# One layout of the PSUM banks in a hybrid decoder step: row tiles and chunks in halves of bank pairs, and the last pair's additions off GpSimd

## The chip, the cores and the metric

The kernel runs on one core of one Trainium2 chip. The core has five engines with queues of their own: TensorE (PE, matmuls), VectorE (DVE), ScalarE (ACT), GpSimd (POOL) and SyncE (SP, here only an issuer of transfers). TensorE writes its sums to PSUM, eight banks of 512 float32 values in each of 128 partitions; VectorE and ScalarE read them from there. The metric is the device time of one execution in microseconds (us), as the median of several runs.

## What is computed

One layer of a decoder for 1024 prompt tokens and 8 sample tokens, 1032 columns in all, D = 2048, in float32:

```
h = rmsnorm(x, g_pre)
proj = h @ w_in
q, k, v, za, ub, zb, ga, gb = split(proj)
ya, s_ret_new = retention(q, k, v, pos, s_ret)
ya = (ya * silu(za)) @ w_pa
yb, s_re_new, s_im_new = s5(ub, s_re, s_im, ...)
yb = (yb * silu(zb)) @ w_pb
merged = sigmoid(ga) * ya + sigmoid(gb) * yb
out = merged @ w_out
return x + rmsnorm(out, g_post), s_ret_new, s_re_new, s_im_new
```

The S5 branch holds one more matrix product, `y * sigmoid(y @ w_glu + b_glu)`. The results are the output rows of both groups and the new states.

## The kernel before

Every float32 factor is split into two parts, `hi` (rounded) and `lo` (the rest), and a product is the sum of three matmuls: hi by hi, hi by lo, lo by hi. For weights this is done by `wtile` and `prep`: SP loads a block of 128 x 512, ACT casts it to `whi`, DVE subtracts to get `wlo`. Both rotate through three buffers.

The work is laid out by hand in program order; a scheduler keeps the order of each engine's queue close to it and puts in the waits. The function `emit` holds it all. Its stages, in order, with what they take from PSUM:

- Start: the first two row tiles of ub, six banks side by side, while x arrives. Then six further row tiles of ub by `linear`. A row tile is 128 output rows by 1032 columns in three thirds of 384, 384 and 264 columns, t = 0, 1, 2; each third takes one bank from `mmbank` and is read by an `evac` function as soon as its last quarter of k is done. Two row tiles of v follow in `ps2`, again six banks.
- The pairs of row tiles of the rest of w_in, then (after the GLU) of w_pa and w_pb. Two row tiles are a 2 x 2 block that is computed with seven products (n = 0 to 6) by the method of Strassen and Winograd. `product` takes a pair of banks for each of three sums, "a", "b" and "d", per step; `evac_st` or `evac_p` reads them. A step has the results "11", "22", "21" and "12": first digit the row tile, second digit the half of the columns. Small additional work is put in between as a background list `bg` (one piece at each `slot`) or at a product's number (`at`, `late_work`).
- The GLU product, eight row tiles by `linear`.
- The out projection. `out_rows` computes the columns from 640 on, 392 wide, with `linear` and `thirds=(3,)`, one bank for each of 16 row tiles. `out_tokens` computes the columns before 640 the other way round, with 128 tokens as rows: three chunks of tokens, then two, in four groups g of 512 output columns, with k in 16 steps and the chunks inside each step. `evac` squares a chunk with ACT, with a misc bank as a place to throw the squares, and multiplies it with DVE.

PSUM has two layouts. `psum_layout(("pmm", 5), ("pms", 3))` gives five single banks for `mmbank` and three for `misc`, which serves transposes and small products. `psum_layout(("pst", 3), ("pms", 2))` gives three pairs and two misc banks. The first holds from the start through the v tiles, the second from the first product to the last one, the first again in the out projection. In the second layout `mmbank` hands out one half of a pair and leaves the other half unused, so that a GLU row tile takes all three pairs.

In the last stage of the pairs, `pb`, the gated result of a pair p is added to what `pa` left in `pap_d`, in `gated`. For p of 0 and 1 the addition is made by an accumulating transfer, and the write to `mg_d` comes LAG = 4 products later. For p over 1 `load_z` loads the other part into a tile `pp` and `add` makes the sum: by DVE, in the last pair (p = 7) by GpSimd for "11", "22" and "21". The second column half of the last two pairs is kept in `last_t` and split (`mg_split`) for the out projection from there; the first half goes through `mg_d`, is loaded again by `fill` and split row by row.

Of the kernel before, what the change touches and what calls it, by code (L numbers as in the profile page):

```python
# [10 lines left out]
F32 = mybir.dt.float32  # L11
# [67 lines left out]
def emit(ctx, tc, I, O):  # L79
    nc = tc.nc  # L80
    V, A, P, T = nc.vector, nc.scalar, nc.gpsimd, nc.tensor

    def tt(out, a, b, op, eng=None):
        return (eng or V).tensor_tensor(out, a, b, op)  # L84
# [4 lines left out]
    def add(out, a, b, eng=None):  # L89
        return tt(out, a, b, ALU.add, eng)  # L90
# [20 lines left out]
    banks_of = {}  # L111

    def psum_layout(*pools):
        if "stack" in banks_of:
            banks_of.pop("stack").close()
            banks_of.clear()
        st = banks_of["stack"] = ExitStack()
        for name, bufs in pools:
            banks_of[name] = st.enter_context(tc.tile_pool(name=name, bufs=bufs, space=PSUM))

    psum_layout(("pmm", 5), ("pms", 3))
    ctx.callback(lambda: banks_of["stack"].close())
    dr = ctx.enter_context(tc.tile_pool(name="dr", bufs=1, space=DRAM))

# [81 lines left out]
    def three(ps, w, i, x, t0, t1, first, last):  # L206
# [3 lines left out]
        T.matmul(ps, wh[:, i, :], xl[:, t0:t1], start=False, stop=False)  # L210
        anchor["p"] = T.matmul(ps, wl[:, i, :], xh[:, t0:t1], start=False, stop=last).ins  # L211

    def mmbank(name="mm"):
        if "pst" in banks_of:
            return banks_of["pst"].tile([128, 2, 512], F32, name="acc")[:, 0, :]
        return banks_of["pmm"].tile([128, 512], F32, name="mm")

    def misc():
        return banks_of["pms"].tile([128, 512], F32, name="misc")
# [8 lines left out]
    def wnext(wd, m, kq):  # L228
        if (m, kq) not in ahead:
            if not todo:  # L230
                return wquarter(wd, m, kq)
            fetch_w()
        if todo:
            fetch_w()
        return ahead.pop((m, kq))

    def linear(wd, m, kt, x, evac, thirds=(0, 1, 2), tick=None):
        ps = {}
        nq = kt // 4
        for kq in range(nq):  # L240
            w = wnext(wd, m, kq)
            for t in thirds:
                t0, t1 = THIRDS[t]
                if kq == 0:
                    ps[t] = mmbank()
                for i in range(4):
                    k = 4 * kq + i
                    three(ps[t][:, 0:t1 - t0], w, i, x(k), t0, t1, k == 0, k == kt - 1)
                if kq == nq - 1:
                    evac(t, ps[t][:, 0:t1 - t0])  # L250
                if tick is not None:
                    tick(kq, t)
            slot()
# [41 lines left out]
    def x_of(k):  # L295
        return xs[k][:, 0, :], xs[k][:, 1, :]
# [49 lines left out]

    with tc.tile_pool(name="start", bufs=3) as sp:
        ssq = sp.tile([128, TOK], F32, name="ssq", bufs=1)
        banks = [[mmbank() for _ in range(3)], [mmbank(), mmbank(), misc()]]
        w = None  # L350
        sqs = deque()
        for k in range(KD):
            xr = sp.tile([128, TOK], F32, name="xr")
            xh, xl = x_of(k)
            parts = THIRDS[0:3] if k == 0 else [(0, TOK)]
            for n, (a, b) in enumerate(parts):
                nc.sync.dma_start(xr[:, a:b], I["xT"][k, :, a:b])
                if k % 4 == 0 and n == 0:
                    w = [wquarter(w_in, M_UB, k // 4)]
                if k % 4 == 0 and n == len(parts) - 1:  # L360
                    w.append(wquarter(w_in, M_UB + 1, k // 4))
                A.activation(xh[:, a:b], xr[:, a:b], AF.Copy, scale=gpre[:, k:k + 1])
                V.scalar_tensor_tensor(xl[:, a:b], xr[:, a:b], gpre[:, k:k + 1], xh[:, a:b].bitcast(F32), ALU.mult, ALU.subtract)  # L363
            if k == 0:
                A.activation(ssq, xr, AF.Square)
            else:
                sqs.append(sp.tile([128, TOK], F32, name="sq", bufs=3))
                A.activation(sqs[-1], xr, AF.Square)
            for j in range(2):
                for t, (t0, t1) in enumerate(THIRDS[0:3]):  # L370
                    three(banks[j][t][:, 0:t1 - t0], w[j], k % 4, x_of(k), t0, t1, k == 0, k == KD - 1)
            if k > 1:
                add(ssq, ssq, sqs.popleft())
        add(ssq, ssq, sqs.popleft())
        for j in range(2):
            for t, (t0, t1) in enumerate(THIRDS[0:3]):
                evac_ub_raw(j, t, banks[j][t][:, 0:t1 - t0])

        def first_rms():
            yield  # L380
            yield from rms_bcast(ssq, rstd, sp)
            for j in range(2):
                scale_ub(j)

        bg.append(first_rms())
        linear(w_in, M_UB + 2, KD, x_of, evac_ub(2))
        drain()

# [424 lines left out]
    steps = [(kh, p) for kh in range(2) for p in range(NP)] + [(kh, p) for kh in ("pa", "pb") for p in range(8)]  # L813
# [63 lines left out]
    acc = {}  # L877
# [298 lines left out]
                yield  # L1176

    bg.append(first_forms())
    ps2 = [[mmbank() for _ in range(3)], [mmbank(), mmbank(), misc()]]
    with tc.issue_after(anchor["s"]):  # L1180
        fetch(0)
    for part_ in range(2):
        for j in range(2):
            for kq in (2 * part_, 2 * part_ + 1):
# [3 lines left out]
                for t, (t0, t1) in enumerate(THIRDS[0:3]):  # L1188
                    for i in range(4):
                        k = 4 * kq + i  # L1190
# [2 lines left out]
                        evac_v(j)(t, ps2[j][t][:, 0:t1 - t0])  # L1193
                slot()
    prep(1)
    psum_layout(("pst", 3), ("pms", 2))
    k2p = {}
    TAGS = [12, 13, 14, 15] + list(range(12))
    xs = {}
# [44 lines left out]
    for s in range(2 * NP):  # L1244
        kh, p = steps[s]
# [235 lines left out]
    zq = {}  # L1481
# [3 lines left out]
    def load_z(s, name):  # L1485
        kind, p = steps[s]
        r, c = AT[name]
        zq[name] = zz_tile()
        A.dma_start(zq[name], (sga_d if kind == "pa" else sgb_d)[2 * p + r, :, HT * c:HT * c + HT])
        if kind == "pb" and p > 1:  # L1490
            zq[name, "p"] = ppp.tile([128, HT], F32, name="pp")
            A.dma_start(zq[name, "p"], pap_d[2 * p + r, :, HT * c:HT * c + HT])

    def gated(g, name, t, ps=None):
        s = g // 7
        kind, p = steps[s]
        r, c = AT[name]
        m, cols = 2 * p + r, slice(HT * c, HT * c + HT)
        z = zq.pop(name)
        if ps is None:  # L1500
            mul(t, t, z)
        else:
            mul(two(t), ps, two(z))
        if kind == "pa":
            P.dma_start(pap_d[m, :, cols], t)
        elif (name, "p") in zq:
            add(t, t, zq.pop((name, "p")), P if p == 7 and name != "12" else V)
            if c and p > 5:
                last_t[m] = t
            P.dma_start(mg_d[m, :, cols], t)  # L1510
        else:
            P.dma_start(t, pap_d[m, :, cols], accum_op=ALU.add)
            at(g + LAG, lambda: P.dma_start(mg_d[m, :, cols], t))
# [45 lines left out]
    for s in range(S0, len(steps)):  # L1559
        kind, p = steps[s]  # L1560
# [57 lines left out]
    estack.close()  # L1618
    wstack.close()
    stage_pool(SW, 3)  # L1620
    psum_layout(("pmm", 5), ("pms", 3))
    zp = ctx.enter_context(tc.tile_pool(name="zp", bufs=1))
    stl = ctx.enter_context(tc.tile_pool(name="stl", bufs=2))
    wxp = ctx.enter_context(tc.tile_pool(name="wxp", bufs=1))
# [79 lines left out]
    def out_tokens(c0, nch, last):  # L1704
# [60 lines left out]
        order_w = deque((g, k) for g in range(4) for k in range(KD))  # L1765
        w = {}
        for g in range(4):
            ps = [mmbank() if c < 2 else misc() for c in range(nch)]
            steps = [[(k, c) for c in range(nch)] for k in range(KD)]
            if last and g == 3:  # L1770
                steps[13:] = [[(k, c) for k in (13, 14, 15)] for c in range(nch)]
            for st in steps:
                for k, c in st:
                    while order_w and order_w[0] <= (g, k + 1):
                        gk = order_w.popleft()
                        w[gk] = wtile(I["w_outB"][gk])
                    wh, wl = (t.rearrange("p a b -> p (a b)") for t in w[g, k])
                    t = (c0 + c) * 128
                    xh, xl = (a[:, t:t + 128] for a in mg[k])
                    for a, b in ((xh, wh), (xh, wl), (xl, wh)):  # L1780
                        anchor["p"] = T.matmul(ps[c], a, b, start=k == 0 and a is xh and b is wh, stop=k == KD - 1 and a is xl).ins  # L1781
                    if k == KD - 1:
                        if c == 0:
                            slots[g] = free.popleft()
                            zt[g] = flat(slots[g])
                            if not last:
                                load_step(g)
                            elif g:
                                for cc in range(nch):
                                    load_x(g, cc)  # L1790
                        evac(g, c, ps[c])
                        if last and g == 3:
                            for gg in range(4):
                                finish(gg, c, A if gg % 2 else nc.sync)
                slot()
# [87 lines left out]
```

## Time and profile before

| | us |
|---|---|
| median of three runs | 2620.34 |
| lowest and highest | 2619.47, 2620.56 |
| the profiled execution | 2618.49 |
| its span, first to last instruction | 2616.7 |

The mean granted TensorE clock of the profiled execution is 0.998 of full speed. The profile is read by its page (busy time of each engine, the costliest groups of instructions, transfers), by its list of waits (for each waiting instruction what ended the wait), by its timeline (start and duration of each instruction, with the idle time before it on its engine in brackets), and by a table of windows (busy time, clock and share of transfers in each stretch). In the tiles' names buffer numbers are left out: `mm`, `misc` and `acc` are PSUM banks, `a` is a split activation, `p`, `u` and `st` are the results of a step on their way out.

### The profile page before, as it was taken

To read this page: it belongs to the slowest core of one execution; us is meant where nothing else is said; L and a number is where in the kernel's file an instruction comes from. 1 tells how busy PE (TensorE), PEld (TensorE's weight loads), DVE (VectorE), ACT (ScalarE), POOL (GpSimd) and SP (SyncE) were. 2 spreads that over 40 slices of the span, in tenths; PEclk is the share of its full clock that TensorE was granted. 3 is DMA by queue.
4 is the path that set the end of the run, shared out by engine and by line. 5 is a ranking of instruction groups with operands and counts; after the bars stand their busy time and mean duration, and the time that the engine had idled before them with its cause. 6 is when DMAs were issued, how large, how long until landed. Compare 5 with 4: busy or idle time off the path is not lost. (4 is left out here: it accounts for less than half of the span.)

```text
span 2616.7 us, 51319 instructions
## 1 busy us (share of the span) xinstructions
PE 2592.8 (99%) x19652; PEld 2531.2 (97%) x19652; DVE 1855.9 (71%) x3872; ACT 955.0 (36%) x1679; POOL 688.8 (26%) x1137
## 2 busy tenths in 40 slices
PE   9999999999999999999999999999999999999998
PEld 8999999999999999999999999999999999998886
DVE  6655988888889877558877666665577877544555
ACT  6113233333323324442234444445332422443344
POOL 0103322222222222332235433333422221111011
PEclk9999999999999999999999999999999999999999
DMA  6896534444444447887778878778867786656666
GB/s 192 262 263 213 154 114 127 138 119 121 133 122 128 131 135 237 206 207 169 166 200 242 228 188 210 200 195 248 271 217 259 231 231 212 216 167 179 188 200 228
DMA packets 229909, 500.25 MB, mean 191 GB/s; under 512 B 32432, under 2 KB 54912, under 8 KB 229536
## 3 DMA queue, kind: packets, MB, share of 16 engines
q0 software_dynamic: 90352, 263.82, 35.9%
q1 hardware_dynamic: 103072, 179.57, 22.5%
q10 hardware_dynamic: 36240, 53.60, 7.0%
q8 instruction: 154, 2.52, 0.4%
q14 instruction: 91, 0.75, 0.1%
HBM read 340.57 MB, written 156.30 MB: 190 GB/s over the span
## 5 line engine op out<-in xcount | busy, mean ns | idle before, releaser
L892 PE MATMUL acc<-a,whi 128*128 128x258 f32 x9632 | 1562.9, 284 | 1.0 <-ACT whi L873 0.6
L892 PEld LDWEIGHTS acc<-a,whi 128*128 128x128 f32 x9632 | 1326.8, 190 | 5.2 <-issue 2.4
L892 PE MATMUL acc<-a,wlo 128*128 128x258 f32 x4816 | 969.5, 283 | 0.0
L892 PEld LDWEIGHTS acc<-a,wlo 128*128 128x128 f32 x4816 | 745.1, 189 | 0.0
L84 DVE TENSOR_TENSOR wlo<-wraw,whi 128x512 fp32r<-128x512 f32 x482 | 332.3, 690 | 235.3 <-ACT whi L202 135.6
L873 ACT CAST whi<-wraw 128x512 fp32r<-128x512 f32 x344 | 213.5, 621 | 619.0 <-PE acc L892 492.5
L873 ACT CAST whi<-wr 128x512 fp32r<-128x512 f32 x258 | 160.1, 620 | 516.8 <-PE acc L892 438.1
L209 PE MATMUL mm<-a,whi 128*128 128x384 f32 (+2 forms) x704 | 233.7, 333 | 8.4 <-ACT whi L202 5.0
L210 PE MATMUL mm<-a,whi 128*128 128x384 f32 (+2 forms) x704 | 233.7, 332 | 0.0
L211 PE MATMUL mm<-a,wlo 128*128 128x384 f32 (+2 forms) x704 | 232.4, 330 | 0.0
L84 DVE TENSOR_TENSOR wlo<-wr,whi 128x512 fp32r<-128x512 f32 x273 | 187.4, 686 | 47.7 <-ACT whi L873 29.8
L1781 PE MATMUL mm<-whi,a 128*128 128x512 f32 x512 | 171.2, 395 | 0.0
L202 ACT CAST whi<-wraw 128x512 fp32r<-128x512 f32 x138 | 85.5, 620 | 210.4 <-PE mm L210 102.4
L209 PEld LDWEIGHTS mm<-a,whi 128*128 128x128 f32 x704 | 133.2, 190 | 9.1 <-ACT whi L202 5.0
L211 PEld LDWEIGHTS mm<-a,wlo 128*128 128x128 f32 x704 | 133.9, 190 | 0.4 <-DVE wlo L84 0.2
L210 PEld LDWEIGHTS mm<-a,whi 128*128 128x128 f32 x704 | 133.4, 189 | 0.4 <-DVE a L363 0.4
L84 DVE TENSOR_TENSOR wraw<-wr 128x512 f32<-128x512 f32 x172 | 118.3, 688 | 6.9 <-DMA wr<-in_w_pa 4.6
L1781 PEld LDWEIGHTS mm<-whi,a 128*128 128x128 f32 x512 | 96.2, 188 | 22.8
L84 DVE TENSOR_TENSOR p<-acc,p 128x516 f32<-128x516 f32 x86 | 59.7, 694 | 77.8 <-PE acc L892 77.6
L84 DVE TENSOR_TENSOR wlo<-wx,whi 128x512 fp32r<-128x512 f32 x76 | 52.5, 692 | 71.0 <-ACT whi L202 70.4
L84 DVE TENSOR_TENSOR u<-acc,u 128x516 f32<-128x516 f32 x86 | 59.7, 694 | 59.5 <-PE acc L892 58.2
L1781 PE MATMUL mm<-wlo,a 128*128 128x512 f32 x256 | 101.4, 396 | 0.0
(374 smaller groups left out, 3416.9 us busy)
## 6 DMA issues: line engine op xcount, KB each, us to landing
wr<-in_w_in SPq DMA_DIRECT2D x280, 256.0 KB
pt_d<-u POOLq DMA_DIRECT2D x70, 258.0 KB, 3.2
u<-pt_d POOLq DMA_DIRECT2D x70, 258.0 KB, 5.3
wraw<-in_w_outB SPq DMA_DIRECT2D x66, 256.0 KB
stg<-fm_d POOLq DMA_DIRECT2D x44, 258.0 KB, 4.3
wx<-in_w_outB SPq DMA_DIRECT2D x43, 256.0 KB
wraw<-in_w_out SPq DMA_DIRECT2D x39, 256.0 KB
pt_d<-st POOLq DMA_DIRECT2D x35, 258.0 KB, 3.4
```

Source lines behind the costliest of these rows:

```text
L84: return (eng or V).tensor_tensor(out, a, b, op)
L202: anchor["a"] = A.copy(hi, raw).ins
L209: T.matmul(ps, wh[:, i, :], xh[:, t0:t1], start=first, stop=False)
L210: T.matmul(ps, wh[:, i, :], xl[:, t0:t1], start=False, stop=False)
L211: anchor["p"] = T.matmul(ps, wl[:, i, :], xh[:, t0:t1], start=False, stop=last).ins
L873: anchor["a"] = A.copy(hi, f).ins
L892: anchor["p"] = T.matmul(ps[:, j, 0:258], a[:, i, :], b[:, 258 * j:258 * j + 258], start=first and i == 0 and a is wh and b is xh, stop=n ...
L1781: anchor["p"] = T.matmul(ps[c], a, b, start=k == 0 and a is xh and b is wh, stop=k == KD - 1 and a is xl).ins
```

## The change

One layout, three pairs and two misc banks, holds for the whole program, and the calls that switch it are gone. `mmbank` takes a pair and hands out its two halves one after the other. `linear` drops an unused half before t = 0, before t = 2 and before t = 3, so that t = 0 and 1 share a pair and the others have one for themselves. The start and the two v tiles take three whole pairs. In `out_tokens` all chunks take halves, also the third that had a misc bank; and in the part with three chunks the last two k are done chunk by chunk.

In the last pair of `pb`, "11" and "21" no longer load `pp` but take the accumulating transfer with its later write to `mg_d`; "22" is added by DVE, as "12" was.

```diff
-    psum_layout(("pmm", 5), ("pms", 3))
+    psum_layout(("pst", 3), ("pms", 2))
...
+    halves = deque()
+
     def mmbank(name="mm"):
-        if "pst" in banks_of:
-            return banks_of["pst"].tile([128, 2, 512], F32, name="acc")[:, 0, :]
-        return banks_of["pmm"].tile([128, 512], F32, name="mm")
+        if not halves:
+            pair_ = banks_of["pst"].tile([128, 2, 512], F32, name="acc")
+            halves.extend((pair_[:, 0, :], pair_[:, 1, :]))
+        return halves.popleft()
...
                 if kq == 0:
+                    if t in (0, 2, 3):
+                        halves.clear()
                     ps[t] = mmbank()
...
-        banks = [[mmbank() for _ in range(3)], [mmbank(), mmbank(), misc()]]
+        banks = [[mmbank() for _ in range(3)] for _ in range(2)]
...
-    ps2 = [[mmbank() for _ in range(3)], [mmbank(), mmbank(), misc()]]
+    halves.clear()
+    ps2 = [[mmbank() for _ in range(3)] for _ in range(2)]
...
     prep(1)
-    psum_layout(("pst", 3), ("pms", 2))
...
-        if kind == "pb" and p > 1:
+        if kind == "pb" and p > 1 and (p < 7 or c):
             zq[name, "p"] = ppp.tile([128, HT], F32, name="pp")
...
-            add(t, t, zq.pop((name, "p")), P if p == 7 and name != "12" else V)
+            add(t, t, zq.pop((name, "p")), V)
...
     stage_pool(SW, 3)
-    psum_layout(("pmm", 5), ("pms", 3))
...
         for g in range(4):
-            ps = [mmbank() if c < 2 else misc() for c in range(nch)]
+            halves.clear()
+            ps = [mmbank() for c in range(nch)]
             steps = [[(k, c) for c in range(nch)] for k in range(KD)]
             if last and g == 3:
                 steps[13:] = [[(k, c) for k in (13, 14, 15)] for c in range(nch)]
+            elif not last:
+                steps[14:] = [[(k, c) for k in (14, 15)] for c in range(nch)]
```

## The prediction

> **What bounds the kernel now.** The page comes first, for the share of the engines:
>
> ```profile
> span 2616.7 us, 51319 instructions
> ...
> PE 2592.8 (99%) x19652; PEld 2531.2 (97%) x19652; DVE 1855.9 (71%) x3872; ACT 955.0 (36%) x1679; POOL 688.8 (26%) x1137
> ```
>
> TensorE (PE) is busy for all but 2616.7 - 2592.8 = 23.9 us. The change removes no matmul, so its gain lies in those 23.9 us and in stretches where PE is busy at a lower clock. The second view is the list of waits, cut to PE. Its columns are the waiting instruction, what came last before it went on, the us in total, the number of times, and the longest:
>
> ```profile
> PE mm L209 <- ACT whi L202: 5.0, 1, 5.0
> PE mm L209 <- DVE u L84: 2.8, 1, 2.8
> PE acc L209 <- ACT p L1423: 1.4, 1, 1.4
> PE mm L209 <- ACT a L362: 0.6, 1, 0.6
> PE acc L892 <- ACT whi L873: 0.6, 1, 0.6
> PE acc L892 <- DVE u L84: 0.4, 2, 0.2
> ```
>
> These are 10.8 us; nearly all the rest lies behind the last matmul (2604.28, last fence), which the change leaves as it is. The 5.0 and the first 0.6 are the start, where PE waits for its first loads. So 2.8, 1.4, 0.6 and 0.4 are left, and the third view, the timeline around each, tells what they wait for.
>
> **Term a, from the v tiles to the first product.** Columns: start, duration, engine, line, operation, tiles, and in brackets the idle time before and its releaser.
>
> ```profile
> 228.76 0.62 ACT L873 CAST whi<-wr 128x512 fp32r<-128x512 f32 x1 [5.09 <-PE mm L210]
> ...
> 239.69 0.28 PE L210 MATMUL misc<-a,whi 128*128 128x264 f32 x1
> 239.81 0.28 PE L211 MATMUL misc<-a,wlo 128*128 128x264 f32 x1
> ...
> 240.13 0.43 DVE L84 TENSOR_TENSOR st<-misc,rstd 128x264 f32<-128x264 f32 x1 [0.90 <-PE misc L211]
> ...
> 240.71 0.72 PE L892 MATMUL acc<-a,whi 128*128 128x258 f32 x4 [0.62 <-ACT whi L873]
> ```
>
> Matmuls of this width follow each other at 0.12 us, so the product could have begun at 239.93; it began at 240.71, 0.78 us late. The releaser named is a cast, but the first product's weights were cast at 228.76. What ends just before 240.71 is the read of the last misc bank (240.13 + 0.43 = 240.56). That bank is not one of the product's own: closing one PSUM layout and opening the next makes the first matmul wait for the last read of any old bank. With one layout the product takes the pair of the first v tile's t = 0 and 1, read one quarter of matmuls earlier. Gain 0.78 us.
>
> **Term b, the second row tile of the GLU matmul.**
>
> ```profile
> 1830.29 0.62 ACT L256 CAST a<-fx 128x516 fp32r<-128x516 f32 x1 [6.62 <-DMA fx<-ya_d]
> ...
> 1832.30 0.68 DVE L84 TENSOR_TENSOR wlo<-wr,whi 128x512 fp32r<-128x512 f32 x1
> ...
> 1833.10 0.28 PE L211 MATMUL acc<-a,wlo 128*128 128x264 f32 x1
> ...
> 1834.15 0.57 ACT L1423 ACTIVATE p<-acc,bglu 128x384 f32<-128x384 f32 x1
> ...
> 1834.78 0.45 PE L209 MATMUL acc<-a,whi 128*128 128x384 f32 x1 [1.40 <-ACT p L1423]
> ...
> 1835.36 0.57 ACT L1423 ACTIVATE u<-acc,bglu 128x384 f32<-128x384 f32 x1
> ```
>
> ScalarE (ACT) stood still until 1830.29 for a transfer, and read the first row's t = 0 late. Before, each of three thirds takes a whole pair of the three, so the second row needs the pair of t = 0 back. After, the first row takes pair 1 (t = 0, 1) and half of pair 2, and the second row begins in pair 3. It can start at 1833.10 + 0.12 = 1833.22 instead of 1834.78: 1.56 us. What is late next: its t = 2 takes pair 1, 24 matmuls at nearly 0.18 us (term c) later, about 1837.4, and the read of t = 1 ends at 1835.93; its weights were there at 1832.98. So all 1.56 us stay.
>
> **Term c, from the last product to the out projection.**
>
> ```profile
> 2234.43 1.14 ACT L202 CAST whi<-wraw 128x512 fp32r<-128x512 f32 x2
> ...
> 2236.44 0.40 PE L892 MATMUL acc<-a,wlo 128*128 128x258 f32 x2
> ...
> 2236.85 1.52 POOL L84 TENSOR_TENSOR p<-p,pp 128x516 f32<-128x516 f32 x1 [1.35 <-DVE p L84]
> 2237.16 1.76 DVE L84 TENSOR_TENSOR wlo<-wraw,whi 128x512 fp32r<-128x512 f32 x1
> ...
> 2238.84 0.68 DVE L84 TENSOR_TENSOR u<-acc,u 128x516 f32<-128x516 f32 x1
> ...
> 2239.67 0.41 PE L209 MATMUL mm<-a,whi 128*128 128x392 f32 x1 [2.83 <-DVE u L84]
> ...
> 2239.92 0.34 PE L210 MATMUL mm<-a,whi 128*128 128x392 f32 x1
> ...
> 2240.10 0.34 PE L211 MATMUL mm<-a,wlo 128*128 128x392 f32 x1
> ...
> 2240.53 0.68 DVE L84 TENSOR_TENSOR wlo<-wraw,whi 128x512 fp32r<-128x512 f32 x1
> ```
>
> The out projection could follow at 2236.68 (two matmuls at 2236.44, 0.12 apart) and began at 2239.67: 2.99 us lost. It waits for the read of the last product (2238.84), a bank that it doesn't need; and that read is late because VectorE (DVE) was held by a wlo that took 1.76 us instead of 0.68 beside GpSimd's (POOL) addition. After, the first pair of the ring is that of the last step's first product, read long before, so the first two matmuls (weights whi, cast by 2235.57) go at once. The third needs wlo: with no addition beside it that ends at 2237.16 + 0.69 = 2237.85, against 2237.04 when PE wants it (matmuls of this width follow each other at 0.18, 2239.92 to 2240.10), so 0.9 us stay lost with the handover. The second quarter's wlo comes after three DVE operations (the read, a split, the gate product, 0.68 + 0.55 + 0.68) at about 2240.2, PE wants it at 2240.1: another 0.2. Gain 2.99 - 1.1 = 1.9 us; bounds 0.9 (that wlo put behind the read) and 2.99.
>
> **Term d, the clock after that gap.** The view by windows (PE busy, granted clock, DMA share, GB/s):
>
> ```profile
> 2237.10:2240.50 3.40, 0.83 (x5) 1.00 0.23 80
> 2240.50:2243.90 3.40, 3.40 (x12) 0.51 0.65 220
> ```
>
> After 3.4 us with PE busy for only 0.83, the next 3.4 us run at a clock of 0.51: 0.49 x 3.40 = 1.67 us of matmul time lost. With 1.1 us of idle time left, in two parts, I expect no drop: gain 1.6 us. The Trainium skill, page "TensorE: Matmul & The Clock Gate", section "Why this matters for your kernels", says that gaps up to about 3 us are harmless and that one whole idle window (3.4 us) halves the clock; by that, the 2.83 us gap here would not have been the cause and d would be nothing. The trace disagrees: the drop follows this gap at once, and the measurement decides.
>
> **What is added or moved, and its cover.** (1) In the last pair the addition of "22" moves from POOL to DVE: 0.69 us more for DVE, beside products that keep PE busy until 2236.8, while three POOL additions go, the last of which stretched that wlo by 1.1 us. Taken at nothing. (2) "11" and "21" lose a load of pp on ACT's queue and get an accumulating DMA on POOL's queue, and their write to mg_d comes four products later or at the end. Its price by the rows of the same kinds of transfer:
>
> ```profile
> u<-pt_d POOLq DMA_DIRECT2D x70, 258.0 KB, 5.3
> ```
>
> ```profile
> 2242.11 0.54 POOL L1510 DMA_DIRECT2D mg_d<-u  x1 [2.89 <-DVE u L84]
> ...
> 2245.95 0.54 POOL L1633 DMA_DIRECT2D z<-in_g_post_row  x1 [3.30 <-DMA mg_d<-u]
> 2246.11 0.81 ACTq L1650 DMA_DIRECT2D z<-mg_d  x2
> ```
>
> "21" is gated by 2236.8; accumulated at 2242.1; written by about 2246.0 (the write issued at 2242.11 took 3.8 us). Behind it stand the load of g_post on POOL, for which nobody waits soon, and whatever z tile lies in the memory of p, among them perhaps the two loads that ACT issues at 2246.11; behind these on ACT is a weight cast of row 1, second quarter. PE wants that 60 matmuls at 0.18 us after 2237.9, at 2248.7; the chain 2246.1 + 0.8 + 0.62 + 0.69 gives 2248.2. Nothing, by 0.5 us; up to 1.5 us if a transfer is slow. (3) The token chunks take three halves instead of two mm and one misc bank, and the last two k go chunk by chunk, which lets the first chunk be read 12 matmuls (2.8 us) before the group ends but holds two weights to the end.
>
> ```profile
> 2412.92 0.62 ACT L202 CAST whi<-wraw 128x512 fp32r<-128x512 f32 x1 [1.48 <-PE misc L1781]
> ...
> 2414.57 0.39 PE L1781 MATMUL misc<-whi,a 128*128 128x512 f32 x1
> ...
> 2414.80 0.39 PE L1781 MATMUL mm<-whi,a 128*128 128x512 f32 x1
> ```
>
> Here the cast for k = 1 of the next group follows the last use of k = 14, 1.9 us before the group's end at 2414.80. After, that use ends three matmuls of 0.23 us, 0.7 us, before the end: cast and wlo are done at about +0.8, PE wants them at +2.1. Nothing; 0.6 us at three boundaries at worst. (4) Two misc banks instead of three, and six halves instead of five banks and a misc at the start: PE shows no wait for a bank there, and the halves are read in the order in which they are taken again. Nothing.
>
> **Sum.** 0.78 + 1.56 + 1.9 + 1.6 = 5.8 us. The profiled execution took 2618.49 us, 1.85 below the median of 2620.34; it would come to 2612.7, and the median to 2620.34 - 5.8 = 2614.5. A measurement of this kernel can tell about 0.2%, 5.2 us: the forecast lies just beyond.
>
> **Rivals.** *No clock gain:* whether the gap costs the clock depends on where it lies in the clock's windows, and the timed runs may not hold the drop, or one may come elsewhere. Then 0.78 + 1.56 + 1.9 = 4.2: 2616.1. For it: the timed runs vary by 1.1 us, and a loss of 1.6 us can hide in them; against: the row above. *A new wait at the out projection:* ACT stands behind a z tile that the accumulated "21" holds, the casts come late, PE idles 1.5 to 2 us there, and c and d shrink to about 1: 2617. For it: the margin of 0.5 us; against: it needs the memory of p under those z tiles. *Waits by pair, not by bank (slower):* if a matmul into one half waits for the read of the other half, then at each row tile and chunk the second half waits once:
>
> ```profile
> L1724 ACT ACTIVATE misc<-mm 128x512 f32<-128x512 f32 x16 | 9.3, 582 | 3.5 <-PE mm L1781 3.0
> ...
> L84 DVE TENSOR_TENSOR z<-mm,z 128x512 f32<-128x512 f32 x16 | 10.6, 687 | 1.7 <-ACT misc L1724 1.5
> ```
>
> 16 row tiles (6 of ub, 2 of v, 8 of the GLU) at about 0.57 and 8 groups of chunks at 0.58 + 0.69 make 19 us, less 5.8: 2634. It decides from the first row tile on. For it: a layout's wait does reach across banks (term a). Against: that is the closing of a pool, and the two bank halves are addressed apart. *Not what it seems:* the first matmuls wait for something else that ends then, and only the POOL additions count: 2619.
>
> **How the numbers follow.** Forecast 0.50 (2612.9 to 2616); no clock gain 0.20; new wait 0.12; by pair or another new wait in the loops 0.10; not what it seems 0.08. Range: low end c at its upper bound and a us of scatter, 2620.34 - 7.9 = 2612.4, say 2612.0; high end 2620.0, over the new wait and most of the last case. Faster by over 0.2% (below 2615.1): most of the forecast case and a little of the others, 0.44; slower, over 2625.6: 0.11; within: 0.45.
>
> **What would show it.** PE's list of waits without "mm L209 <- DVE u" and "acc L209 <- ACT p" (b, c), the first product 0.12 us after the last v matmul (a), no slice with a clock near 0.5 at 2240 (d), the wlo at 0.69 us there; nothing new at L1781. It is wrong if PE waits inside a row tile for its own pair, if a new wait of over 1 us stands at the out projection, or if the sum of PE's waits falls and the time doesn't.
>
> ```profile
> 2604.28 0.40 PE L1781 MATMUL mm<-whi,a 128*128 128x512 f32 x1
> ```
>
> From there to the end the rows should be the same.

## The result and the profile after

The changed kernel is slower. Its median is 2632.16 us (2629.80 to 2635.22, four runs) against 2619.90 for the kernel before (four runs, the three above and one more): ratio 1.0050, interval 1.0038 to 1.0062. The forecast was 2614.5, with a range up to 2620.0. The profiled execution took 2633.15 us.

The page's busy times of the engines come first:

```profile
span 2631.4 us, 51316 instructions
...
PE 2599.2 (99%) x19652; PEld 2530.6 (96%) x19652; DVE 1852.7 (70%) x3873; ACT 954.8 (36%) x1679; POOL 686.2 (26%) x1136
```

The span is 14.7 us longer. PE stands idle for 2631.4 - 2599.2 = 32.2 us, 8.3 more than before, and is busy for 6.4 more with the same matmuls, so part of the loss is in the clock or in waits too short to show as idle time. The list of PE's waits says where:

```profile
PE acc L209 <- DVE ubp L84: 7.3, 5, 5.2
PE acc L209 <- ACT whi L202: 4.9, 1, 4.9
PE acc L209 <- ACT p L1428: 3.1, 1, 3.1
PE misc L1054 <- ACT a L1052: 2.3, 1, 2.3
PE acc L1788 <- DVE z L84: 1.5, 1, 1.5
PE acc L897 <- DVE u L84: 1.0, 3, 0.7
```

The 4.9 is the old wait for the first loads, and the waits that terms b and c counted on removing have new ones beside or instead of them. Two are new in kind: matmuls of `linear` wait for the read `ubp` (the row tiles of ub), and a matmul of the token chunks waits for `z`. A third, for the read `p` (the GLU), stands in place of the old one of 1.4, at another matmul. The same list for the weight loads (PEld) is finer. It holds short waits that PE's list doesn't have:

```profile
PEld acc L209 <- DVE ubp L84: 8.6, 6, 5.4
PEld acc L209 <- ACT p L1428: 4.4, 8, 3.3
PEld acc L1788 <- DVE z L84: 4.0, 8, 1.9
```

Six and eight are the numbers of the row tiles that `linear` makes of ub and of the GLU: one wait in each. Of the eight in the chunks, seven lie in the groups of three chunks and one at the very end. Before, `ubp` and `z` don't appear in this list, and `p` once with 1.6. That is the mark of the rival *waits by pair*. The v tiles show no such wait: in the trace the first seven matmuls of the first product run ahead of the last twelve of the v tiles, so the read has time.

How much time each stage lost is read from the trace by the start of the same instruction in both profiled executions:

| stage | before | after | difference |
|---|---|---|---|
| start to the sixth product step (its first read of a sum by ACT) | 344.99 | 356.14 | +11.15 |
| from there to the first GLU matmul | 1476.92 | 1480.14 | +3.22 |
| GLU | 92.12 | 95.16 | +3.04 |
| products of pa and pb | 325.64 | 322.65 | -2.99 |
| out rows | 139.42 | 137.80 | -1.62 |
| token chunks to the last matmul | 225.19 | 229.01 | +3.82 |
| last matmul to the end | 12.42 | 10.50 | -1.92 |

The largest loss is one stall at the second row tile of ub that `linear` makes, the fourth of all. This is its timeline in the changed kernel:

```profile
100.10 1.29 DVE L771 SCALAR_TENSOR_TENSOR fx<-fx,g_pre,rstd 128x1032 f32<-128x1032 f32 x1 [4.44 <-DMA fx<-in_xT]
...
102.85 0.28 PE L211 MATMUL acc<-a,wlo 128*128 128x264 f32 x1
...
106.20 0.62 ACT L202 CAST whi<-wraw 128x512 fp32r<-128x512 f32 x1 [10.95 <-DMA fm_d<-fx]
...
106.85 0.69 DVE L84 TENSOR_TENSOR wlo<-wraw,whi 128x512 fp32r<-128x512 f32 x1 [2.31 <-ACT whi L202]
107.46 0.79 DVE L84 TENSOR_TENSOR ubp<-acc,rstd 128x384 f32<-128x384 f32 x1
108.31 0.69 PE L209 MATMUL acc<-a,whi 128*128 128x384 f32 x1 [5.17 <-DVE ubp L84]
```

PE wants to begin the last quarter of t = 1 at about 103.1 and has its weights and its columns. It waits for DVE's read of t = 0, the other half of its own pair. That read stands in DVE's queue behind a `wlo`, which waits for a cast of ACT, which waited 10.95 us behind transfers of the `fm_d` forms. None of this has to do with t = 1. In the kernel before, the same read stood behind the same chain, and came no sooner than PE was done with t = 1 either:

```profile
101.85 0.62 ACT L202 CAST whi<-wraw 128x512 fp32r<-128x512 f32 x1 [8.15 <-DVE fo L84]
102.50 0.69 DVE L84 TENSOR_TENSOR wlo<-wraw,whi 128x512 fp32r<-128x512 f32 x1 [1.35 <-ACT whi L202]
103.11 2.03 DVE L84 TENSOR_TENSOR ubp<-mm,rstd 128x384 f32<-128x384 f32 x5
```

Nobody waited for it there, as t = 1 had a bank of its own. The chain itself is some 4 us later in the changed kernel, from a later load of `fx`; with the read at 103.11, as before, the wait would have been under 1 us (an estimate: the read takes 0.79, and PE wants to begin at 103.1). The lateness comes with the sharing: the scaling of `fx` begins at 100.10 here and at 99.19 in e5 below, which shares its pairs in the same way, and between 94.34 and 96.49 in the kernel before and in the seven experiments whose row tiles of ub don't wait inside a pair. What makes it late was not traced. For the changed kernel the windows (PE busy, clock, DMA share, GB/s) show what follows:

```profile
103.00:106.40 3.40, 0.13 (x2) 0.91 1.05 371
106.40:109.80 3.40, 1.50 (x5) 0.50 1.07 239
109.80:113.20 3.40, 3.40 (x16) 0.59 0.91 254
```

After a window with hardly a matmul, two run at a clock of 0.50 and 0.59: 1.50 x 0.50 + 3.40 x 0.41 = 2.1 us lost on top of the 5.17. With the 2.1 us of the other `ubp` waits in PE's list this makes 9.4 of the 11.15; by the weight loads' list it is 8.6 + 2.1 = 10.7.

In the GLU the same wait takes the place of the one removed:

```profile
1844.87 0.28 PE L210 MATMUL acc<-a,whi 128*128 128x264 f32 x1
...
1847.05 0.62 ACT L261 CAST a<-fx 128x516 fp32r<-128x516 f32 x1 [1.13 <-DVE fx L84]
1847.58 0.58 ACT L1428 ACTIVATE p<-acc,bglu 128x384 f32<-128x384 f32 x1
1848.20 0.45 PE L209 MATMUL acc<-a,whi 128*128 128x384 f32 x1 [3.05 <-ACT p L1428]
```

Before, the second row tile waited 1.40 us for ACT's read of t = 0. Now the first row tile's own t = 1 waits for that read, which has four casts ahead of it on ACT, for 3.05.

The token chunks end with the third place. The last chunk but one is finished at about 2617.4 (2617.03 + 0.39); the last chunk's remaining nine matmuls can't start until both its reads are done:

```profile
2617.03 0.39 PE L1788 MATMUL acc<-whi,a 128*128 128x512 f32 x1
2617.46 0.58 ACT L1728 ACTIVATE misc<-acc 128x512 f32<-128x512 f32 x1 [1.54 <-PE acc L1788]
...
2618.18 0.69 DVE L84 TENSOR_TENSOR z<-acc,z 128x512 f32<-128x512 f32 x1 [1.54 <-ACT misc L1728]
...
2618.93 0.50 PE L1788 MATMUL acc<-whi,a 128*128 128x512 f32 x1 [1.50 <-DVE z L84]
```

Part of this is given back behind the last matmul (-1.92 in the table): DVE has finished the other chunk by then, and its read of the last chunk starts 1.38 us after the last matmul (2622.28) where it started 3.15 us after it before (2607.43). The prediction had taken the rows behind the last matmul as unchanged. For the stage of the chunks the weight loads' list gives the size: 4.0 us of waits for `z` against +3.82.

The out projection did what the forecast hoped, and more:

```profile
2253.59 1.29 DVE L84 TENSOR_TENSOR wlo<-wraw,whi 128x512 fp32r<-128x512 f32 x2
2253.85 0.40 PE L897 MATMUL acc<-a,wlo 128*128 128x258 f32 x2
2254.09 0.34 PE L209 MATMUL acc<-a,whi 128*128 128x392 f32 x1
...
2254.45 0.34 PE L211 MATMUL acc<-a,wlo 128*128 128x392 f32 x1
```

It follows the last product at 0.12 us, and the `wlo` is ready in time (the pair ends at 2254.88, its first by 2254.28, wanted at 2254.45).

### The profile page after: what moved, and what is told of

The parts are those of the page before. It is cut to its first block, busy times and chain, and to the rows that moved or that the text cites. A ratio compares the mean times of both kernels' runs of the same rounds, so it can differ in the third digit from the quotient of the medians.

```text
span 2631.4 us, 51316 instructions
## 1 busy us (share of the span) xinstructions
PE 2599.2 (99%) x19652; PEld 2530.6 (96%) x19652; DVE 1852.7 (70%) x3873; ACT 954.8 (36%) x1679; POOL 686.2 (26%) x1136
## 5 line engine op out<-in xcount | busy, mean ns | idle before, releaser
L897 PEld LDWEIGHTS acc<-a,whi 128*128 128x128 f32 x9632 | 1326.7, 190 | 5.9 <-issue 3.0
L897 PEld LDWEIGHTS acc<-a,wlo 128*128 128x128 f32 x4816 | 744.7, 189 | 0.0
L209 PE MATMUL acc<-a,whi 128*128 128x384 f32 (+2 forms) x928 | 306.5, 331 | 15.6 <-DVE ubp L84 7.3
L210 PE MATMUL acc<-a,whi 128*128 128x384 f32 (+2 forms) x928 | 304.0, 328 | 0.1
L211 PE MATMUL acc<-a,wlo 128*128 128x384 f32 (+2 forms) x928 | 301.9, 326 | 0.1
L1788 PE MATMUL acc<-whi,a 128*128 128x512 f32 x640 | 202.2, 396 | 1.5 <-DVE z L84 1.5
L209 PEld LDWEIGHTS acc<-a,whi 128*128 128x128 f32 x928 | 175.4, 189 | 19.2 <-DVE ubp L84 8.6
L211 PEld LDWEIGHTS acc<-a,wlo 128*128 128x128 f32 x928 | 175.9, 190 | 0.9 <-DVE wlo L84 0.7
L210 PEld LDWEIGHTS acc<-a,whi 128*128 128x128 f32 x928 | 175.7, 189 | 0.7 <-DVE a L368 0.7
L1788 PEld LDWEIGHTS acc<-whi,a 128*128 128x128 f32 x640 | 120.2, 188 | 32.2 <-DVE z L84 4.0
L1788 PE MATMUL acc<-wlo,a 128*128 128x512 f32 x320 | 126.9, 397 | 0.1
L84 DVE TENSOR_TENSOR u<-acc,p 128x516 f32<-128x516 f32 x86 | 59.5, 692 | 59.8 <-PE acc L897 59.4
```

Of the source, the lines that this page charges most:

```text
L209: T.matmul(ps, wh[:, i, :], xh[:, t0:t1], start=first, stop=False)
L897: anchor["p"] = T.matmul(ps[:, j, 0:258], a[:, i, :], b[:, 258 * j:258 * j + 258], start=first and i == 0 and a is wh and b is xh, stop=n ...
```

## The experiments

The runs of the kernel before that stand beside the three sets of experiments have medians of 2619.90, 2618.43 and 2617.89 us. So each experiment is compared with its own, by the ratio, and a difference between two experiments of different sets is good to about 2 us.

**What orders the waits.** In the program, a pair is one tile. The program's list of PE instructions with their waits, for the row tile of ub with the stall above, shows the wait at the first matmul of the last quarter of t = 1 in the changed kernel (`acc_849` is the pair of t = 0 and 1), and none for the same matmul before, where each third has its own tile:

```
before: 564 L209 MATMUL mm_866<-a12_117,whi_1001 128x384
after:  564 L209 MATMUL acc_874<-a12_117,whi_996 128x264
        570 L209 MATMUL acc_849<-a12_117,whi_996 128x384 [waits DVE_49]
```

(The row of before is that of `mm_866`, the bank of t = 1; row 564 of the changed kernel is the first of t = 2's last quarter.) The count of DVE's semaphore that row 570 waits for is the one that DVE's read of t = 0, the other half of `acc_849`, sets.

In the changed kernel the order is different, too: half of the last quarter of t = 2 (the 264 wide matmuls) is put ahead of that of t = 1. That covers the wait where the read is prompt, which fits the sizes: most of the waits are 0.2 to 0.7 us. It was to be shown that this wait is the cause, and not the number of banks (three pairs in place of eight single ones), the additions, or the order of the chunks.

**e1, the read behind both halves.** All of the change stays; only the reads of two halves are moved behind the matmuls of both, so that no matmul of a pair has a read of that pair ahead of it. The last group of chunks can't wait that long and takes a pair for each chunk.

```diff
-                if kq == nq - 1:
-                    evac(t, ps[t][:, 0:t1 - t0])
+                if kq == nq - 1 and t:
+                    for e in (0, 1) if t == 1 else (t,):
+                        evac(e, ps[e][:, 0:THIRDS[e][1] - THIRDS[e][0]])
...
-                        evac(g, c, ps[c])
+                        split_ = last and g == 3
+                        for e in (c,) if split_ or c > 1 else (0, 1) if c else ():
+                            evac(g, e, ps[e])
```

The v tiles are treated in the same way, and `halves.clear()` stands ahead of each chunk's `mmbank` in that last group.

> Layout and additions as in the changed kernel; only the place of the reads in program order differs: a half of a pair is read after the matmuls of both halves (row tiles of ub, v and GLU, and the token chunks; the chunks of the last group get a pair each). Theory 'waits by pair' (a matmul into one half waits for a read of the other half that stands before it in program order): PE's waits for ubp (7.3 us in 5) and for the sigmoid p (3.1) and the one at L1788 (1.5) go, and with the first the 6.8 us at half clock; 2614 to 2617. Rival 'too few banks' (three pairs give less room than five single banks when DVE is late behind its transfers): the 5 us wait at the third ub row and the clock drop stay, 2627 to 2632. Rival 'order of the queues' (the reads stand behind the building of the forms for another reason): same, 2627 to 2632.

Measured: 2612.01 us, ratio 0.9975 (0.9965 to 0.9985) against 2618.43 for before on that chip. That is some 20 us below the changed kernel, with the same layout and the same additions, clear of both kernels and 2 us below what was expected of the theory. All of the new waits are gone from PE's list:

```profile
PE acc L209 <- ACT whi L202: 4.9, 1, 4.9
PE acc L898 <- DVE u L84: 0.4, 2, 0.2
PE acc L209 <- ACT a L368: 0.2, 1, 0.2
```

At the place of the stall DVE reads t = 0 and 1 together, no sooner than in the kernel before (103.11), and PE goes on:

```profile
103.09 0.28 PE L211 MATMUL acc<-a,wlo 128*128 128x264 f32 x1
103.12 1.50 DVE L84 TENSOR_TENSOR ubp<-acc,rstd 128x384 f32<-128x384 f32 x2
103.20 0.28 PE L209 MATMUL acc<-a,whi 128*128 128x264 f32 x1
```

**e2, the same in `linear` alone.** Only the first hunk of e1; the v tiles and the chunks are as in the change.

> The changed kernel with the reads moved behind both halves in the row tiles of ub (from the third) and of the GLU alone; the v tiles and the token chunks read as in the changed kernel. Theory 'waits by pair': the waits for ubp and p go, the one at L1788 stays, and the token chunks keep their 2 us (last matmul 3.8 us later after the first chunk than before, the end 1.9 us): 2613.5 to 2615. Rival (the chunks' loss came of the late start): 2612, as with all reads moved.

Measured: 2614.57 us, ratio 0.9988 (0.9979 to 0.9997). The row tiles of ub and the GLU carry most of the loss. The weight loads of the chunks still have the eight waits, the same 4.0 us in all as in the changed kernel:

```profile
PEld acc L1789 <- DVE z L84: 4.0, 8, 1.9
```

**e3, the start in the old layout.** `mmbank` gives single banks up to the v tiles, and the layout is switched ahead of the products, as before; the rest is the change.

```diff
-    psum_layout(("pst", 3), ("pms", 2))
+    psum_layout(("pmm", 5), ("pms", 3))
...
+        if "pmm" in banks_of:
+            return banks_of["pmm"].tile([128, 512], F32, name="mm")
...
+    psum_layout(("pst", 3), ("pms", 2))
```

> The start through the two v tiles in the old layout (five single banks and three misc), everything behind it as in the changed kernel. Theory 'waits by pair': the first product begins at about 240.7 again instead of 249.6, the waits in the GLU (3.1) and at L1788 (1.5) stay; if the 4.3 us that the steps between lose come of other things than the start, 2632 - 9 = 2623; if they come of the start's lateness, 2619. Rival (the loss is spread over the program and not the start's): 2628 or more.

Measured: 2621.65 us, ratio 1.0011 (1.0002 to 1.0020): about 10.5 us less than the changed kernel, in line with the 11.15 of the first stage, and between the two values of the expectation. The GLU and the chunks still wait, 4.0 us (3.1 in the changed kernel) and 1.5.

**e4, the additions alone.** The kernel before with the last pair's additions off GpSimd, in the old layout.

```diff
-        if kind == "pb" and p > 1:
+        if kind == "pb" and p > 1 and (p < 7 or c):
...
-            add(t, t, zq.pop((name, "p")), P if p == 7 and name != "12" else V)
+            add(t, t, zq.pop((name, "p")), V)
```

> The kernel before with the edit of the additions alone (accumulating transfers for 11 and 21, 22 on DVE), both layouts kept. Theory: the wlo before the out projection takes 0.69 instead of 1.76 us, the gap there shrinks from 2.8 to about 1.8 us and the clock may not drop: 2616.5 to 2619. Rival (no part of the gap hangs on it): 2619.9.

Measured: 2615.65 us, ratio 0.9988 (0.9979 to 0.9997), some 1 us below the expected range. The wait at the out projection falls from 2.8 to 1.4 us and the clock drop behind it is gone (the clock is 1.00 in all 3.4 us windows from 2229 to 2246):

```profile
PE mm L209 <- DVE u L84: 1.4, 1, 1.4
PE acc L209 <- ACT p L1423: 0.9, 1, 0.9
```

**e5, the layout alone.** The change with the two lines of e4 put back as they were.

> The changed kernel without the edit of the additions: one layout, GpSimd adds in the last pair as before. Theory: no wait for the read of the last product at the out projection, but a wlo that is 1.1 us late beside the additions: 0 to 2 us more than the changed kernel, 2632 to 2634. If the gain of 3 us at that place is the additions' and not the layout's: the gap of 2.8 us is there again, with a clock drop, 2636.

Measured: 2634.76 us, ratio 1.0061 (1.0048 to 1.0074), at the upper end of what was expected. The layout alone makes the loss. The additions may take about 2.9 us off it by the two ratios, but their intervals overlap. The profiles show it at its place: the out rows take 141.41 us here and 137.80 in the changed kernel. With GpSimd's addition there the `wlo` is late, even though no old bank is waited for:

```profile
2251.84 1.52 POOL L84 TENSOR_TENSOR p<-p,pp 128x516 f32<-128x516 f32 x1 [1.34 <-DVE p L84]
2252.15 1.75 DVE L84 TENSOR_TENSOR wlo<-wraw,whi 128x512 fp32r<-128x512 f32 x1
...
2253.96 0.45 PE L211 MATMUL acc<-a,wlo 128*128 128x392 f32 x1 [1.77 <-DVE wlo L84]
```

**e6, the moved reads with GpSimd's additions.** e1 with the same two lines put back.

> All reads moved, one layout, but the additions of the last pair on GpSimd as before. Theory: the wlo of the out projection's first quarter is late by 1.1 to 1.8 us beside the additions (1.8 in the run of the layout alone, with a clock drop of 3.4 us behind it): 2613 to 2616. Rival (with the layout the additions no longer matter): 2612.

Measured: 2614.43 us, ratio 0.9987 (0.9979 to 0.9996), some 3 us above e1 by the two ratios (their intervals overlap in part). The same wait for the `wlo` stands there, 1.8 us, without a clock drop this time; the out rows take 139.99 us against 137.80 in e1. So the additions and the layout are both needed at the out projection: the layout removes the wait for an old bank, and the additions the late `wlo` that would come next. In the profiles, from the GLU's end to the end of the out rows, e4 (additions alone) takes 3.0 us less than the kernel before, e6 (layout alone, reads moved) 2.4, and e1 4.6.

**e7, the chunks in their old order.** e1 without the edit that takes the last two k chunk by chunk.

```diff
-            elif not last:
-                steps[14:] = [[(k, c) for k in (14, 15)] for c in range(nch)]
```

> All reads moved, but in the part with three chunks the last two k go k by k as before. Theory: the pair of the first two chunks is read 2.8 us later against the next group, whose third chunk needs it after 1.4 us; a squares pass of 0.78 and a product of 0.69 for each of two chunks make PE wait 0.5 to 1.5 us at three boundaries: 2613.5 to 2616. Rival (the scheduler finds other matmuls for the gap): 2612.

Measured: 2612.32 us, ratio 0.9978 (0.9969 to 0.9987), against 0.9975 for e1. The rival was right and the theory of waits at three boundaries wrong. Once the reads are moved that edit has no effect that can be measured.

**e8, a pair for every third.** The change with each third of a row tile in a pair of its own, whose other half is left empty; the reads are where the change has them.

```diff
                 if kq == 0:
-                    if t in (0, 2, 3):
-                        halves.clear()
+                    halves.clear()
```

> The changed kernel, reads where they were, but each third of a row tile takes a pair of its own (its second half unused), also in ub. No pair is shared in a row tile, so 'waits by pair' has nothing to act on there; what is left is the number of banks. GLU as before (wait of 1.4 us). In ub a row needs the pair of the same third of the row before: with the reads at about 103 to 108 us, late behind the forms, PE waits 2 to 5 us at the third ub row if the number of banks matters too, then 2618 to 2626; if sharing was all of it, no wait for ubp and 2616.

Measured: 2618.39 us, ratio 1.0004 (0.9995 to 1.0013), some 12 us below the changed kernel by the two ratios, with half of each pair of a row tile left empty. Were the small ring the cause, this would have been the worst of all. Its list of waits has what is left:

```profile
PE acc L1787 <- DVE z L84: 1.5, 1, 1.5
PE acc L209 <- DVE ubp L84: 1.3, 1, 1.3
PE acc L209 <- ACT p L1427: 0.4, 1, 0.4
```

Here `ubp` is a wait at the first matmul of a row tile, for a pair of the row tile before, which is the price of a ring of three: 1.3 us at one place. The expectation for sharing alone, no wait for `ubp` and 2616, was missed by that and by about 1 us more. The chunks, which e8 leaves as the change has them, wait as in the changed kernel.

## Why the prediction was wrong, step by step

**The step that failed** is the assumption, made in term b and parts (3) and (4) of what is added, that a half of a pair can be written while the other half waits for its read. It was put as an argument against the right rival: "the two bank halves are addressed apart". They are, but the waits are put in for the tile, and the tile is the pair. The row of term a that was quoted (a layout's wait reaching across banks) spoke for it, and so did the kernel itself: every pair that the kernel before read had both its halves written first, so its trace couldn't show the case. A change that makes two accumulations share one tile with a read between them had no row behind it, and it was taken at nothing. It cost some 20 us (2632.16 against 2612.01 in e1), against a forecast gain of 5.8. The prediction's own sign of being wrong, PE waiting inside a row tile for its own pair, is what the list of waits shows.

The wait is one that the program puts in, as its list of instructions shows. No run read one half of a pair while the other was written, so no run shows what would happen without the wait. In the kernel before, though, DVE reads the bank of t = 0 from 103.11 while matmuls go into that of t = 2. The Trainium skill, page "PSUM — Partial Sum Buffer", section "PSUM bank collisions raise a hardware error", has accesses of two engines to different banks run clean, and asks for a guard by bank and quadrant, or more simply by bank.

**The rival's price** was 19 us, and the changed kernel lies 20 us above e1. That its size came out is luck, since its way there was another. It had 24 waits of 0.57 to 1.27 us, spread evenly; in the trace most are far shorter, covered by the change of order. The weight loads' 22 waits add up to 8.6 + 4.4 + 4.0 = 17.0 us, of which three make 5.4 + 3.3 + 1.9 = 10.6, and 2.1 us come from the clock. These three are where the read comes late: behind transfers at the start, behind casts in the GLU, and at the end behind the chain of square and product.

**Term a** (0.78): right. In e1 the first product starts at 239.98, 0.73 earlier than before. In the changed kernel it also follows its forerunner without a gap, at 249.61 after a matmul at 249.43; but there twelve matmuls of the v tiles come behind it, where the prediction had it follow the last of them:

```profile
249.61 0.66 PE L897 MATMUL acc<-a,whi 128*128 128x258 f32 x4
...
250.47 0.35 PE L209 MATMUL acc<-a,whi 128*128 128x264 f32 x1
```

**Term b** (1.56): right in size once the pair's wait is gone: the GLU takes 90.52 us in e1, 1.60 less than before. "So all 1.56 us stay" was wrong for the change as made: what was late next was the row tile's own t = 1, which was not looked at.

**Term c** (1.9, bounds 0.9 and 2.99): at its upper bound. The products to the out projection take 2.99 us less, in the changed kernel and in e1. The term assumed that the `wlo` would start where it started before, at 2237.16, behind the same work; but without the additions two `wlo` run together, ahead of the end of the products. e6 shows the other case: with GpSimd's addition a wait of 1.8 us stays.

**Term d** (1.6): right, 1.62 in the changed kernel and in e1, where no wait is left there. e4, which only halves that wait, has 1.56 too (137.86 against 139.42). That the 1.1 us of idle time which the prediction left there would have cost no clock is not shown: a wait of 1.8 us had no drop behind it in e6 and one in e5.

**The edits costed at nothing.** (1) and (2), the additions and the accumulating transfer, cost nothing that can be seen: PE has no wait at the out projection, so the margin of 0.5 us for the cast held. They are worth 2.9 and 3.1 us by the two comparisons of ratios (e5 to the change, e6 to e1), neither clear of noise. (3) is nothing as an order of the chunks (e7), but the halves of the chunks cost about 2 us: in the profiles the chunks and the end take 1.9 us more in e2 than in e1 (239.46 against 237.52). The other 1.7 of the 3.6 us between their spans lie ahead of the GLU, where e2 leaves the v tiles as the change has them. (4) is where nothing was most wrong: 11.15 us in the first stage.

**The sum.** 5.8 us was forecast and e1 is 6.4 below before (2618.43 - 2612.01; by the ratio's interval, 3.9 to 9.2). The terms describe e1, which is the change with its reads in another place. It beats both kernels.

**What stays open.** The table's +3.22 lies mostly at the retention's first head, where an activation table load waits for a transfer; in the profiles of the other runs, e5 with the same layout among them, that wait isn't in the list, and one execution each doesn't say why. Of the first stage's 11.15 us the waits and the clock explain 9.4 to 10.7; the rest was not traced. Two tiles in place of a pair, which would let each half have waits of its own, weren't tried.

## What to carry to other kernels

Two accumulations that share one tile share its waits: a read of the one holds back the next matmul of the other. Before putting two in one tile, go through each and ask whether a read of the first stands before a matmul of the second in program order, and what that read stands behind on its own engine; if it does, move the read behind both. When a bank plan looks free because no wait shows in the profile of before, check that the profile contains the case at all.

## What the hardware showed that was not expected

**The clock drop doesn't follow the length of the gap alone.** A gap of 2.83 us (before) was followed by 3.4 us at 0.51, one of 5.17 by 0.50 and 0.59; one of 3.05 in the GLU was followed by none:

```profile
1844.50:1848.00 3.50, 0.65 (x6) 1.00 1.04 363
1848.00:1851.40 3.40, 3.19 (x19) 1.00 1.03 371
```

The clearest pair is the same wait of 1.8 us in e5 and in e6. In e5 it is followed by half the clock:

```profile
2251.80:2255.20 3.40, 1.63 (x10) 1.00 0.12 44
2255.20:2258.60 3.40, 3.40 (x12) 0.50 0.66 236
```

In e6 it isn't:

```profile
2234.80:2238.20 3.40, 1.62 (x9) 1.00 0.18 58
2238.20:2241.60 3.40, 3.40 (x20) 1.00 0.68 231
```

PE's busy time in the window is the same (1.63 and 1.62). What differs may be where the gap falls in time, which would fit a clock that judges by windows of its own; that is an inference, as no run moved the gap on purpose. The Trainium skill, page "TensorE: Matmul & The Clock Gate", says in its section "Why this matters for your kernels" to avoid gaps of more than about 3 us; the drops behind 1.77 us in e5 and 2.83 us before came at shorter gaps than that.

**A GpSimd addition holds up VectorE until past the addition's end.** The prediction had read the slow `wlo` off one row. It comes again in the two experiments that keep the addition: an addition of two inputs on GpSimd (in e5's rows above 1.52 us from 2251.84) stretches a VectorE subtraction of two inputs that begins 0.31 us after it to 1.75 us in e5 and 1.76 in e6. In the changed kernel, which differs from e5 in the additions alone, two such subtractions take 1.29 together. The stretched one ends 0.54 us after the addition in e5 and 0.55 in e6 and before.
